# Conditioning rows loaded on GpSimd's queue into a buffer of their own, and reduced across four stages of a mixer block

## The chip, the cores and the metric

One core of one Trainium2 chip. The metric is the device time of one execution in microseconds (us), taken as the median of several runs. Engines: PE (TensorE), DVE (VectorE), ACT (ScalarE), POOL (GpSimd), SP (SyncE, which here only issues DMAs). Each engine runs its instructions in the order in which they stand in its own queue.

## The reference

One layer of a diffusion backbone. Input: 512 latent tokens of width 1024, 256 context tokens, and a conditioning vector c. What matters here:

```
mod = split(silu(c) @ w_ada + b_ada, 6)          # six vectors of 1024
h   = rms_norm(x) * (1 + mod[1]) + mod[0]         # the same for the context tokens
z, xbc, dt, cv, pool, gates = split(h @ w_in)
xbc = silu(conv5(xbc) + bias)                     # 1536 channels, 5 taps
y   = ssd_scan(xbc, dt) from the context's final states, both directions
y   = rms_norm(y * silu(z)) @ ssd_w_out
merged = sum over 3 branches of sigmoid(gates[b]) * branch[b]
x   = x + mod[2] * (merged @ w_out)
h   = rms_norm(x) * (1 + mod[4]) + mod[3]
x   = x + mod[5] * swiglu(h)
out = rms_norm(x)
```

Of the context tokens only xbc's first ten channel tiles and dt are needed, for the states from which the latent scan starts.

## The kernel before, in words

**Products.** Channels lie on the 128 partitions, tokens along the free axis. A unit of weights is a tile of 128 x 1024 fp32 (512 KB), eight blocks of 128 columns, and gives one output tile of 128 channels x 512 tokens. Every operand is kept as a pair hi, lo whose sum is the fp32 value, and `mm3` (L132 to L137) makes a product of three matmuls per block: hi by hi (L135), hi by lo (L136), lo by hi (L137). `load_unit` (L116 to L127) issues the DMA of a unit into one of three buffers `wr` (L113, on SP's queue), casts it to `whi` on ACT (L121) and takes the difference `wlo` on DVE (L123).

**Order.** A tile framework schedules the instructions by dependence and by a running priority. Code under `later(n)` gets a later priority, so that work of one stage can stand as filler in another; buffers of a pool (the last argument of `pt`) bound how far an instruction moves up.

**Stages.** Start, GLU and pool branch (to about 165 us); twelve xBC units; the SSD scan, with z and gate units as filler for PE; gates, layer norm of the convolution branch and its output units `wcv` (to 517.6 us); the units `wso` with the merge of the three branches; the units `wout` with the residual; the FFN from 605 us and its down projection.

**xBC unit** (loop at L721). 24 matmuls of 512 tokens for the latent tokens; in the first ten units 24 more of 256 for the context tokens, against `hc`, the context's pairs hi, lo of 128 x 256. ACT copies both results into a padded tile `pad` (slots C5, four of them), whose edges POOL clears (L727, L728, L734). `conv5` makes four taps on DVE (L669), ACT applies Silu, and the tail (`xbc_tail`, a generator) transposes the result on PE (L699, L703), scales a part on DVE (L706) and multiplies it on PE (L715). The tail of one unit stands inside the next but one. `conv_steps` adds taps of the 31 tap convolution (L403) as filler for DVE.

**Conditioning.** Chunks 2, 4 and 3 of mod are not needed until `wout` and later. `ada()` (L854 to L863) makes 128 values of them: it loads a tile of 512 KB of `wada` with `load_raw`, so into a shared buffer `wr` on SP's queue, and one DVE instruction (L861) multiplies it by silu(c) and sums along the free axis into a column of `mod_l`. 24 such calls stand in the gate units (4), the `wcv` units (4), the `wso` units (8) and the `wout` units (8). Eight more, of chunk 5, stand in the down projection.

**Merge.** In each `wso` unit m SP loads gate tile m (`ga`, L933) and the two spilled branch results (`mo`, L934) from DRAM, 512 KB each; DVE combines them with the product (L936 to L939) and splits the result for `wout`.

Of the kernel before, what the change touches and what calls it, by code (L numbers as in the profile page):

```python
# [8 lines left out]
F32 = mybir.dt.float32  # L9
F32R = mybir.dt.float32r  # L10
AF = mybir.ActivationFunctionType
ALU = mybir.AluOpType
P = 128
# [39 lines left out]
def hybrid_block(ctx, tc, x, cx, cck, cc, wad, wada, vec, prm, cst, inv, win, wdt, wcv, wpl, wso, wout, wgu, wdn, out):  # L53
# [78 lines left out]
    def mm3(o, w, col, rhs, first, last):  # L132
        hi, lo = w
        rh, rl = rhs
        PE.matmul(o, hi[:, col : col + P], rh, start=first, stop=False)  # L135
        PE.matmul(o, hi[:, col : col + P], rl, start=False, stop=False)  # L136
        PE.matmul(o, lo[:, col : col + P], rh, start=False, stop=last)  # L137
# [272 lines left out]
    def conv_steps(n, ins=None):  # L410
        with ExitStack() as st:
            st.enter_context(later(100000))
            if ins is not None:
                st.enter_context(tc.issue_after(ins.ins))
            while n and convs:
                if next(convs[0], 0) == 0:
                    convs.popleft()
                else:
                    n -= 1
# [87 lines left out]
    def ctx_norm():  # L507
        x3 = xc[:, 0:2, :].rearrange("p a (t n) -> p (a t) n", n=TC)
        nc.sync.dma_start(x3, cx)
        xs_c = [x3[:, t, :] for t in range(KT)]  # L510
        r = norm_sum(xs_c, TC)
        hq = [slot_h([P, 4, 2, TC], F32R) for _ in range(2)]
        for t in range(KT):
            h = hq[t // 4][:, t % 4]
            make_h(xs_c[t], r, m1_c[:, t : t + 1], mod_c[:, t : t + 1], h[:, 0, :], h[:, 1, :])
            hc.append((h[:, 0, :], h[:, 1, :]))

    def pool_all():
        plp, waiting = [], []
# [155 lines left out]
    def xbc_tail(i, pad):  # L675
# [17 lines left out]
        else:  # L693
# [23 lines left out]
                    )  # L717
            S.copy(pinit[:, :, i * P : (i + 1) * P], st[:, :TC].rearrange("p (d n) -> p d n", n=P))

    tails = []  # L720
    for q, i in enumerate((8, 9, 10, 11, 0, 1, 2, 3, 4, 5, 6, 7)):  # L721
        w = load_unit(win[I_XBC + q])
        o = mmp()
        for k in range(KT):
            mm3(o, w, k * P, hh[k], k == 0, k == KT - 1)
        pad = slot_c()
        nc.gpsimd.memset(pad[:, 0:2], 0.0)  # L727
        nc.gpsimd.memset(pad[:, 514:518], 0.0)  # L728
        S.copy(pad[:, 2:514], o)
        if i < 10:  # L730
            oc = mmp()
            for k in range(KT):
                mm3(oc[:, :TC], w, k * P, hc[k], k == 0, k == KT - 1)
            nc.gpsimd.memset(pad[:, 774:776], 0.0)  # L734
            S.copy(pad[:, 518:774], oc[:, :TC])
        conv_steps(CONV_STEPS_XBC[q], mark[-1])
        while len(tails) > TAILS_KEPT_XBC[q]:
            drain(tails.pop(0))
        tails.append(xbc_tail(i, pad))
        next(tails[-1], None)  # L740
# [99 lines left out]
            nc.sync.dma_start(yd[:, 4 * g : 4 * g + 4, zs], zc)  # L840
            yield

    silb = [None]

    def load_sil(t):
        nc.sync.dma_start(t, cc[0:1, :].to_broadcast([P, 1024]))
        tc.keep_in_program_order(S.activation(t, t, AF.Silu))
        silb[0] = t

    adas = deque()  # L850
    for i in range(24):
        adas.append(((2, 4, 3)[i // 8], i % 8))

    def ada(n=1):  # L854
        for _ in range(n):
            if not adas:
                return
            chunk, t = adas.popleft()
            raw = load_raw(wada[(chunk - 2) * 8 + t], 1024)
            i = chunk * 8 + t  # L860
            V.tensor_tensor_reduce(  # L861
                raw, raw, silb[0], 1.0, vc("b_ada", i), ALU.mult, ALU.add, mod_l[:, i : i + 1]
            )  # L863

    load_sil(f1.tile([P, 1024], F32, tag="sil1", name="sil1"))
    gens = [ssd_gen(0), ssd_gen(1)]
    for g in gens:
        next(g)
# [58 lines left out]
    for m in range(8):  # L927
        w = load_unit(wso[m])
        o = mmp()
        for k in range(KT):  # L930
            mm3(o, w, k * P, y_hl[k], k == 0, k == KT - 1)
        ga, mo = slot_a(), slot_c().rearrange("p (a b) -> p a b", b=T)
        nc.sync.dma_start(ga, gat[:, m])  # L933
        nc.sync.dma_start(mo, mrg[:, m])  # L934
        S.activation(ga, ga, AF.Sigmoid)
        V.tensor_tensor(mo[:, 1, :], mo[:, 1, :], ga[:, 1, :], ALU.mult)  # L936
        V.tensor_tensor(mo[:, 0, :], mo[:, 0, :], mo[:, 1, :], ALU.add)
        V.tensor_tensor(ga[:, 0, :], o, ga[:, 0, :], ALU.mult)
        V.tensor_tensor(mo[:, 0, :], mo[:, 0, :], ga[:, 0, :], ALU.add)  # L939
        mr = mo[:, 0, :]  # L940
        split(mg[m][0], mg[m][1], mr)
        ada(1)

    x1 = slot_x([P, KT, T])
    acc = pt(per, [P, T], "sum", 1)
# [51 lines left out]
    for m in range(nh):  # L997
        if m < 2:
            o = pair[m][1]
        else:  # L1000
            w, o = wout_tile(m)
            project(o, [(w, KT)], mg, whole[0])
        residual(m, o, mod_l[:, 16 + m : 17 + m], xp[m // 2][:, m % 2, :], whole[0], slot_m())
        prescale(m, whole[0])
        ada(2 - m // 3)
    last = [wout_tile(m) for m in range(nh, 8)]
    h2 = [(pt(per, [P, T], "hh", 8, F32R), pt(per, [P, T], "hl", 8, F32R)) for _ in range(KT)]

# [190 lines left out]
    hid = hs  # L1199

    acc = pt(per, [P, T], "sum", 1)
    for m in range(8):
        ada(1)
        o = mmp()
# [129 lines left out]
```

## Time and profile before

| | |
|---|---|
| median of 3 runs | 979.4 us (977.9 to 980.53) |
| the profiled execution | 976.52 us |
| span in its trace | 974.7 us |
| mean granted clock of PE in the span | 0.996 |
| PE busy | 948.8 us (97%) |
| DVE busy | 764.9 us (78%) |
| ACT busy | 492.2 us (50%) |
| POOL busy | 15.9 us (2%) |
| moved by DMA | 151.67 MB, 156 GB/s over the span |

The span is that of the instructions; the execution's own time is 1.8 us more. The median of the runs is 2.9 us above the profiled execution. A matmul's busy time in a row is its latency; matmuls overlap, so the step from one start to the next tells their rate. The granted clock is written as a share: 1.00 is 2.4 GHz and 0.50 is 1.2 GHz.

### The profile page before, as it was taken

The numbers are of one execution on the slowest core, as the hardware profiler recorded it, in microseconds if no ns is written. First come the engines' busy times: TensorE is split into PE (matmuls) and PEld (weight loads), VectorE is DVE, ScalarE is ACT, GpSimd is POOL, SyncE is SP. The second block draws the span as 40 slices with busy tenths as digits, with TensorE's granted clock in tenths as the row PEclk, the third lists the DMA queues.
The fourth block names the chain that finished last, engine by engine and source line by source line (L and its number), as shares of the span: only waits on it lengthen the run. The fifth ranks groups of instructions, "written<-read, shape, count | busy, mean of one in ns | idle before, by whom it ended". The sixth has DMA issues, their size and how long they took to land.

```text
span 974.7 us, 14173 instructions
## 1 busy us (share of the span) xinstructions
PE 948.8 (97%) x5420; PEld 803.6 (82%) x5420; DVE 764.9 (78%) x1165; ACT 492.2 (50%) x815; POOL 15.9 (2%) x58
## 2 busy tenths in 40 slices
PE   6999999999999999999999989999999999999996
PEld 4678888888887776777888769989999999888885
DVE  5589999967889999987876976999889888643333
ACT  5683597335445254644844434745555556432331
POOL 0000000000000000000000000000000000000000
PEclk9999999999999999999999999999999999999998
DMA  9753455321112346665578984223232323343422
GB/s 364 282 187 110 164 179 173 109 87 65 67 65 76 108 162 195 216 205 196 176 259 318 363 278 170 91 104 131 101 117 87 119 99 122 127 141 109 136 79 87
DMA packets 55492, 151.67 MB, mean 156 GB/s; under 512 B 5760, under 2 KB 16512, under 8 KB 54272
## 3 DMA queue, kind: packets, MB, share of 16 engines
q1 hardware_dynamic: 55424, 150.77, 44.6%
q8 instruction: 42, 0.69, 0.3%
q14 instruction: 26, 0.21, 0.1%
HBM read 134.43 MB, written 16.32 MB: 155 GB/s over the span
## 4 chain that ended last, share of the span: by engine, by line
PE 86%; DVE 7%; DMA 4%; ACT 2%; issue 1%; SPq 0%; DVEq 0%; ACTq 0%
PE mm L137 19%; PE mm L135 19%; PE mm L136 19%; PE mm L1122 10%; PE ps L1122 8%; PE mm L62 1%; DMA C<-mrg 1%; DVE wlo L123 1%; DVE A L403 1%; PE ps L1039 1%; PE ps L763 1%; PE y L825 1%; PE ps L62 1%; PE ps L715 1%; DMA wr<-in_wso_dram 1%
## 5 line engine op out<-in xcount | busy, mean ns | idle before, releaser
L135 PE MATMUL mm<-hh,whi 128*128 128x512 f32 (+1 forms) x612 | 242.4, 396 | 0.0
L137 PE MATMUL mm<-hh,wlo 128*128 128x512 f32 (+1 forms) x612 | 241.2, 394 | 0.5 <-DVE wlo L123 0.5
L136 PE MATMUL mm<-hl,whi 128*128 128x512 f32 x576 | 228.9, 397 | 0.0
L121 ACT CAST whi<-wr 128x1024 fp32r<-128x1024 f32 (+1 forms) x115 | 116.9, 1019 | 212.1 <-PE mm L136 167.4
L123 DVE TENSOR_TENSOR wlo<-wr,whi 128x1024 fp32r<-128x1024 f32 (+1 forms) x112 | 132.2, 1183 | 63.1 <-ACT whi L121 62.0
L137 PEld LDWEIGHTS mm<-hh,wlo 128*128 128x128 f32 x612 | 115.0, 188 | 28.3 <-issue 2.8
L135 PEld LDWEIGHTS mm<-hh,whi 128*128 128x128 f32 x612 | 115.1, 188 | 26.0 <-issue 1.7
L136 PEld LDWEIGHTS mm<-hl,whi 128*128 128x128 f32 x576 | 108.3, 188 | 25.0 <-issue 2.7
L403 DVE SCALAR_TENSOR_TENSOR A<-U,vec_t,A 128x504 f32<-128x504 f32 (+14 forms) x180 | 115.4, 684 | 0.1
L129 ACT CAST shi<-S 128x1024 fp32r<-128x1024 f32 x36 | 37.9, 1052 | 32.1 <-DVE S L1110 26.3
L1122 PE MATMUL mm<-T,shi 128*128 128x256 f32 x288 | 53.5, 283 | 0.0
L669 DVE SCALAR_TENSOR_TENSOR C<-C,vec_t,C 128x772 f32<-128x772 f32 (+1 forms) x48 | 46.9, 977 | 4.9 <-ACT C L667 2.4
L130 DVE TENSOR_TENSOR slo<-S,shi 128x1024 fp32r<-128x1024 f32 x36 | 44.1, 1225 | 5.8 <-ACT shi L129 5.7
L818 ACT ACTIVATE E<-E,sbias 128x128 f32<-128x128 f32 x128 | 40.0, 392 | 10.6 <-DMA E<-cumd 10.5
L1122 PEld LDWEIGHTS mm<-T,shi 128*128 128x128 f32 x288 | 44.8, 191 | 0.0
L129 ACT CAST whi<-wr 128x1024 fp32r<-128x1024 f32 (+1 forms) x36 | 30.0, 835 | 26.0 <-PE ps L1122 21.4
L861 DVE CUSTOM_DVE_ANT_0 wr<-wr,sil,vec_t 128x1024 f32<-128x1024 f32 x24 | 30.8, 1282 | 13.4 <-DMA wr<-in_wada_dram 13.4
L137 PE MATMUL mm<-H,wlo 128*128 128x256 f32 (+1 forms) x124 | 38.0, 307 | 2.9 <-DVE wlo L123 2.8
L1122 PE MATMUL mm<-T,slo 128*128 128x256 f32 x144 | 40.8, 284 | 0.0
L130 DVE TENSOR_TENSOR wlo<-wr,whi 128x1024 fp32r<-128x1024 f32 (+1 forms) x36 | 34.5, 958 | 7.6 <-ACT whi L129 6.0
L135 PE MATMUL mm<-H,whi 128*128 128x256 f32 (+1 forms) x124 | 37.8, 305 | 0.0
L136 PE MATMUL mm<-H,whi 128*128 128x256 f32 (+1 forms) x124 | 37.7, 304 | 0.0
(383 smaller groups left out, 2039.4 us busy)
## 6 DMA issues: line engine op xcount, KB each, us to landing
wr<-in_win_dram SPq DMA_DIRECT2D x62, 512.0 KB, 3.7
wr<-in_wgu_dram SPq DMA_DIRECT2D x44, 512.0 KB, 3.4
wr<-in_wada_dram SPq DMA_DIRECT2D x32, 512.0 KB, 4.0
E<-cumd SPq DMA_DIRECT2D x16, 512.0 KB, 5.3
wr<-in_wdn_dram SPq DMA_DIRECT2D x16, 512.0 KB, 3.9
X<-in_wad_dram SPq DMA_DIRECT2D x4, 1024.0 KB, 10.6
H<-in_wad_dram SPq DMA_DIRECT2D x4, 1024.0 KB, 11.2
mrg<-tmp SPq DMA_DIRECT2D x16, 256.0 KB, 4.0
```

Source lines behind the costliest of these rows:

```text
L121: S.copy(hi[:, :n], raw[:, :n])
L123: V.tensor_tensor(lo[:, :n], raw[:, :n], hi[:, :n], ALU.subtract)
L129: S.copy(dst_hi, src)
L130: V.tensor_tensor(dst_lo, src, dst_hi, ALU.subtract)
L135: PE.matmul(o, hi[:, col : col + P], rh, start=first, stop=False)
L136: PE.matmul(o, hi[:, col : col + P], rl, start=False, stop=False)
L137: PE.matmul(o, lo[:, col : col + P], rh, start=False, stop=last)
L403: V.scalar_tensor_tensor(accs[e][:, :, o], ins[e][:, :, q], vc("dw_w", (2 * j + e) * 31 + 15 + d), accs[e][:, :, o], ALU.mult, ALU.add)
L669: tap = V.scalar_tensor_tensor(a[:, 0:n], pad[:, k : n + k], vc("conv_w", i * 5 + k), a[:, 0:n], ALU.mult, ALU.add)
L818: S.activation(dec[d][:, j, :], dec[d][:, j, :], AF.Identity, bias=sbias[:, z, c : c + 1])
L861: V.tensor_tensor_reduce(raw, raw, silb[0], 1.0, vc("b_ada", i), ALU.mult, ALU.add, mod_l[:, i : i + 1])
L1122: PE.matmul(o[:, left], x[:, cs], rhs[k][y], start=first and k + n == 0, stop=k == 3 and n == 2, skip_group_check=True,)
```

## The change

1. `hc` now holds, for each block of the context, hi (128 x 256) and the whole pair hi, lo side by side (128 x 512). The context product of an xBC unit is then two matmuls per block: whi by the pair (512 columns, L761) and wlo by hi (256 columns, L762). The two halves of the result are added on DVE (L765) as the second goes into `pad`.
2. `ada()` moves ahead of the xBC units. It loads into a buffer `ar` of its own, of which there is one, on GpSimd's DMA queue (L743), and the reduce (L735) of one call is issued by the next call, before its load. Its 24 calls stand in nine xBC units, the gate units (4), the `wcv` units (4) and seven `wso` units. The eight calls of chunk 5 use the same buffer and queue.
3. In the `wso` units `ga` and `mo` are loaded on GpSimd's queue (L941, L942).

```diff
-            hc.append((h[:, 0, :], h[:, 1, :]))
+            hc.append((h[:, 0, :], h.rearrange("p a n -> p (a n)")))
...
+    loaded = []
+
+    def ada_rest():
+        while loaded:
+            i, raw = loaded.pop()
+            V.tensor_tensor_reduce(raw, raw, silb[0], 1.0, vc("b_ada", i), ALU.mult, ALU.add, mod_l[:, i : i + 1])
+
+    def ada(n=1):
+        for _ in range(n):
+            ada_rest()
+            if adas:
+                chunk, t = adas.popleft()
+                raw = pt(per, [P, 1024], "ar", 1)
+                nc.gpsimd.dma_start(raw, wada[(chunk - 2) * 8 + t])
+                loaded.append((chunk * 8 + t, raw))
...
             oc = mmp()
             for k in range(KT):
-                mm3(oc[:, :TC], w, k * P, hc[k], k == 0, k == KT - 1)
+                ks = slice(k * P, k * P + P)
+                PE.matmul(oc, w[0][:, ks], hc[k][1], start=k == 0, stop=False, skip_group_check=True)
+                PE.matmul(oc[:, :TC], w[1][:, ks], hc[k][0], start=False, stop=k == KT - 1, skip_group_check=True)
             nc.gpsimd.memset(pad[:, 774:776], 0.0)
             S.copy(pad[:, 518:774], oc[:, :TC])
+            V.tensor_tensor(pad[:, 518:774], oc[:, TC:], pad[:, 518:774], ALU.add)
         conv_steps(CONV_STEPS_XBC[q], mark[-1])
+        ada(q > 2)
...
-    def ada(n=1):
-        for _ in range(n):
-            if not adas:
-                return
-            chunk, t = adas.popleft()
-            raw = load_raw(wada[(chunk - 2) * 8 + t], 1024)
-            i = chunk * 8 + t
-            V.tensor_tensor_reduce(
-                raw, raw, silb[0], 1.0, vc("b_ada", i), ALU.mult, ALU.add, mod_l[:, i : i + 1]
-            )
...
-        nc.sync.dma_start(ga, gat[:, m])
-        nc.sync.dma_start(mo, mrg[:, m])
+        nc.gpsimd.dma_start(ga, gat[:, m])
+        nc.gpsimd.dma_start(mo, mrg[:, m])
...
-        ada(1)
+        ada(m < 7)
+        if m == 7:
+            ada_rest()
...
-        ada(2 - m // 3)
...
+    ada(1)
     for m in range(8):
         ada(1)
```

The scheduler does not leave the calls where the code has them. Three places show it.

DVE in one xBC unit, before. C is the padded tile or the taps' sum, W the scaled part of the tail, A and U the 31 tap convolution:

```order
L706 TENSOR_TENSOR W_2070<-ps_2067,wdec 128x256
L123 TENSOR_TENSOR wlo_2271<-wr_2268,whi_2270 128x1024
L706 TENSOR_TENSOR W_2070<-ps_2067,wdec 128x256
L669 SCALAR_TENSOR_TENSOR C_315_2079<-C_309_2028,vec_t,C_315_2079 128x772 x4
L403 SCALAR_TENSOR_TENSOR A_457<-U_782,vec_t,A_457 128x8x53
L403 SCALAR_TENSOR_TENSOR A_457<-U_785,vec_t,A_457 128x8x53
L403 SCALAR_TENSOR_TENSOR A_457<-U_782,vec_t,A_457 128x8x52
L403 SCALAR_TENSOR_TENSOR A_457<-U_785,vec_t,A_457 128x8x52
L706 TENSOR_TENSOR W_2161<-ps_2158,wdec 128x256
```

The same place after the change; the reduces are the ISA rows with `ar`, and the ISA row behind each hands on its sum:

```order
L123 TENSOR_TENSOR wlo_2246<-wr_2243,whi_2245 128x1024
L765 TENSOR_TENSOR C_311_2015<-mm_2019,C_311_2015 128x256
L706 TENSOR_TENSOR W_2053<-ps_2050,wdec 128x256 x2
L735 ISA ar_3063,mod_l<-ar_3063,sil_1680,vec_t 128x1024
L735 ISA mod_l 128x1
L669 SCALAR_TENSOR_TENSOR C_318_2062<-C_311_2015,vec_t,C_318_2062 128x772 x4
L735 ISA ar_3202,mod_l<-ar_3202,sil_1680,vec_t 128x1024
L735 ISA mod_l 128x1
L403 SCALAR_TENSOR_TENSOR A_457<-U_782,vec_t,A_457 128x8x53
L403 SCALAR_TENSOR_TENSOR A_457<-U_785,vec_t,A_457 128x8x53
L123 TENSOR_TENSOR wlo_2333<-wr_2330,whi_2332 128x1024
```

Two reduces now stand in the unit, one between the tail (L706) and the taps (L669) of its convolution. In DVE's whole order 21 of the 24 reduces stand between the last rows of the pool branch and the end of the xBC tails, and the other three among the first rows of the SSD scan; none is left in the gate, `wcv`, `wso` or `wout` units.

PE at the border of two xBC units, before, with the tail's transposes (L699, L703):

```order
L136 MATMUL mm_2032<-H_617,whi_1999 128x256
L137 MATMUL mm_2032<-H_617,wlo_2000 128x256
L699 MATMUL ps_2061<-ident,C_304_1990 128x128 x4
L703 MATMUL ps_2067<-ident,C_304_1990 128x128 x2
L135 MATMUL mm_2092<-hh_81,whi_2088 128x512
L136 MATMUL mm_2092<-hl_82,whi_2088 128x512
L137 MATMUL mm_2092<-hh_81,wlo_2089 128x512
L715 MATMUL ps_2073<-W_2070,W_1676 128x128 x2
```

The same place after the change:

```order
L761 MATMUL mm_2104<-H_617,whi_2071 128x512
L762 MATMUL mm_2104<-H_617,wlo_2072 128x256
L135 MATMUL mm_2162<-hh_81,whi_2158 128x512
L136 MATMUL mm_2162<-hl_82,whi_2158 128x512
L137 MATMUL mm_2162<-hh_81,wlo_2159 128x512
L135 MATMUL mm_2162<-hh_83,whi_2158 128x512
L699 MATMUL ps_2131<-ident,C_318_2062 128x128 x4
L703 MATMUL ps_2137<-ident,C_318_2062 128x128 x2
L136 MATMUL mm_2162<-hl_84,whi_2158 128x512
```

The transposes stand four matmuls into the next unit here; in the units that follow, 8 to 12.

POOL in the xBC units after the change, where before it had only the clearings of the pads:

```order
L743 DMA ar_2390<-in_wada_dram 128x1024
L754 MEMSET C_303_1948 128x2
L755 MEMSET C_303_1948 128x4
L763 MEMSET C_303_1948 128x2
L743 DMA ar_2483<-in_wada_dram 128x1024
L754 MEMSET C_311_2015 128x2
L755 MEMSET C_311_2015 128x4
L763 MEMSET C_311_2015 128x2
L743 DMA ar_2570<-in_wada_dram 128x1024
L743 DMA ar_3063<-in_wada_dram 128x1024
```

The single buffer lets each DMA start only after the reduce of the tile before. The clearings of a unit's pad stand behind such DMAs. The first DMA, of `ar_1898`, stands at the head of POOL's queue, before the first clearings of the pool branch, and waits for nothing.

## Rows read from the trace of the kernel before

**Rows 1.** The page's first part: busy time, share, instructions of each engine.

```profile
PE 948.8 (97%) x5420; PEld 803.6 (82%) x5420; DVE 764.9 (78%) x1165; ACT 492.2 (50%) x815; POOL 15.9 (2%) x58
```

**Rows 2.** Windows: stretch, its us, busy of PE, PEld, DVE, ACT, POOL, clock, DMA share, GB/s.

```profile
165.00:320.00 155.00, 155.00 (x843) 131.32 (x842) 130.32 (x178) 66.86 (x101) 2.31 (x35) 1.00 0.23 79
320.00:460.00 140.00, 137.56 (x665) 101.56 (x665) 126.48 (x204) 71.06 (x148) 10.18 (x8) 1.00 0.55 182
...
517.60:565.00 47.40, 45.29 (x195) 35.89 (x193) 40.21 (x61) 22.41 (x26) 0.00 (x0) 1.00 0.94 347
565.00:605.00 40.00, 38.63 (x194) 32.51 (x195) 26.87 (x39) 16.36 (x23) 0.00 (x0) 0.96 0.71 245
```

**Rows 3.** Waits of PE: line, awaited, us in total, times, longest.

```profile
PE mm L137 <- DVE wlo L123: 3.3, 3, 2.0
PE ps L763 <- DVE W L761: 1.6, 1, 1.6
```

**Rows 4.** Timeline of PE around 563 us: start, us, instruction, idle before.

```profile
561.88 0.39 PE L135 MATMUL mm<-hh,whi 128*128 128x512 f32 x1
562.11 0.39 PE L136 MATMUL mm<-hl,whi 128*128 128x512 f32 x1
...
563.03 0.39 PE L136 MATMUL mm<-H,whi 128*128 128x512 f32 x1
565.38 0.50 PE L137 MATMUL mm<-H,wlo 128*128 128x512 f32 x1 [1.96 <-DVE wlo L123]
```

**Rows 5.** Windows, as rows 2: the stretch after that stall.

```profile
566.50:569.80 3.30, 3.30 (x10) 2.58 (x9) 2.72 (x4) 0.80 (x1) 0.00 (x0) 0.52 0.78 284
```

**Rows 6.** DMA issues of 505 to 610: issue, count, KB each, median us to landing.

```profile
wr<-in_wada_dram SPq DMA_DIRECT2D x16, 512.0 KB, 4.6
...
C<-mrg SPq DMA_DIRECT2D x7, 512.0 KB, 6.8
```

**Rows 7.** Chain that ended last, 505 to 612: start, length, what.

```profile
519.51 6.09 DMA C<-mrg
...
543.71 5.76 DMA wr<-in_wso_dram
...
578.96 3.48 DMA wr<-in_wout_dram
```

**Rows 8.** DVE by line and form, 500 to 610: count, busy us, mean ns, idle before.

```profile
L861 DVE CUSTOM_DVE_ANT_0 wr<-wr,sil,vec_t 128x1024 f32<-128x1024 f32 x17 | 21.8, 1282 | 10.8 <-DMA wr<-in_wada_dram 10.8
```

**Rows 9.** Timeline of DVE through one xBC unit: start, us, instruction, idle before.

```profile
282.66 0.42 DVE L706 TENSOR_TENSOR W<-ps,wdec 128x256 f32<-128x256 f32 x1 [1.60 <-PE ps L703]
283.00 1.22 DVE L123 TENSOR_TENSOR wlo<-wr,whi 128x1024 fp32r<-128x1024 f32 x1
284.13 0.42 DVE L706 TENSOR_TENSOR W<-ps,wdec 128x256 f32<-128x256 f32 x1
284.65 4.27 DVE L669 SCALAR_TENSOR_TENSOR C<-C,vec_t,C 128x772 f32<-128x772 f32 x4
288.83 1.16 DVE L403 SCALAR_TENSOR_TENSOR A<-U,vec_t,A 128x392 f32<-128x392 f32 x2
...
292.69 0.42 DVE L706 TENSOR_TENSOR W<-ps,wdec 128x256 f32<-128x256 f32 x1 [1.37 <-PE ps L703]
```

**Rows 10.** DMA issues of 195 to 320, as rows 6.

```profile
wr<-in_win_dram SPq DMA_DIRECT2D x14, 512.0 KB, 3.5
```

**Rows 11.** Timeline of PE, end of a context product.

```profile
251.46 0.28 PE L136 MATMUL mm<-H,whi 128*128 128x256 f32 x1
251.58 0.28 PE L137 MATMUL mm<-H,wlo 128*128 128x256 f32 x1
```

**Rows 12.** Chain that ended last, 0 to 30, as rows 7.

```profile
1.65 5.33 DMA X<-in_wad_dram
```

**Rows 13.** DMA view, 0 to 26 us: GB/s in 40 slices.

```profile
GB/s 0 0 30 131 323 93 403 365 429 321 391 375 394 410 410 407 407 463 432 466 397 384 416 479 403 429 429 429 466 403 397 391 473 416 429 416 416 454 403 435
```

**Rows 14.** POOL by line and form, whole run, as rows 8.

```profile
L795 POOL TENSOR_TENSOR W<-X,cbd 128x512 f32<-128x512 f32 x8 | 10.2, 1272 | 146.5 <-DVE cbd L791 105.3 <-issue 29.7 <-DMA yd<-W 11.5
```

More of the change, by code (lines that the diff above doesn't have):

```diff
@@ L718, in xbc_tail, with load_sil @@
             S.copy(pinit[:, :, i * P : (i + 1) * P], st[:, :TC].rearrange("p (d n) -> p d n", n=P))
+    silb = [None]
+    def load_sil(t):
+        nc.sync.dma_start(t, cc[0:1, :].to_broadcast([P, 1024]))
+        tc.keep_in_program_order(S.activation(t, t, AF.Silu))
+        silb[0] = t
+    adas = deque()
+    for i in range(24):
+        adas.append(((2, 4, 3)[i // 8], i % 8))
+    loaded = []
[11 more added lines that the diff above has]
+                loaded.append((chunk * 8 + t, raw))
+    load_sil(f1.tile([P, 1024], F32, tag="sil1", name="sil1"))
     tails = []
@@ L841, in ssd_gen @@
             yield
[L843 to L852, printed above, removed]
-    def ada(n=1):
-        for _ in range(n):
-            if not adas:
-                return
-            chunk, t = adas.popleft()
-            raw = load_raw(wada[(chunk - 2) * 8 + t], 1024)
-            i = chunk * 8 + t
-            V.tensor_tensor_reduce(
-                raw, raw, silb[0], 1.0, vc("b_ada", i), ALU.mult, ALU.add, mod_l[:, i : i + 1]
-            )
-    load_sil(f1.tile([P, 1024], F32, tag="sil1", name="sil1"))
     gens = [ssd_gen(0), ssd_gen(1)]
```

## The prediction

> **What bounds the kernel now.** I read the page's busy shares first: PE works 948.8 us, 97% of the span [rows 1], so it is the bound, and the change can win only where PE waits, where its clock falls, or where it does less. The waits of PE come next. Apart from the wait for the first weights at the start, only two releasers in the part that the change touches cost more than 1.2 us: the difference `wlo` of a weight unit, 3.3 us in three waits, and a tile W in the SSD scan, 1.6 us [rows 3]. The windows by stage then show who is nearly full behind PE [rows 2]. In the xBC stage (165 to 320) DVE works 130.3 of 155 us and the DMA engines are 23% busy; in the SSD scan DVE works 126.5 of 140 us; in the `wso` stage it is the DMA engines that are full, 94% at 347 GB/s, and in the `wout` stage they are still at 71%.
>
> The three waits for `wlo` all lie in those last two stages. The timeline shows the longest: a matmul at 563.03 us, the next at 565.38, where the step is 0.23 us otherwise [rows 4]. In the stretch behind it the granted clock is 0.52 for 3.3 us, the lower level, and is back before 570 us [rows 5]. The chain through these stages runs over transfers: a branch result `C<-mrg` of 6.1 us, a weight unit of `wso` of 5.8 us, one of `wout` of 3.5 us [rows 7]. Between 505 and 610 us, 16 loads of `wada` (4.6 us each) stand beside the merge's loads (6.8 us) on the same engines [rows 6], and on DVE their reduces stand in the order ahead of `wlo`.
>
> **The change, part by part.** The sum starts from the profiled execution, 976.52 us. That run is 2.9 us below the median of the runs (979.4), so I carry the difference over to the median at the end.
>
> *The start.* The first load of a conditioning row is now at the head of POOL's queue and waits for nothing. The transfers of the start already run at some 410 GB/s [rows 13] and the end's chain begins with one of them [rows 12]. Another 512 KB at that rate is 0.52 MB / 410 GB/s = 1.3 us. It costs nothing if it lands in a gap and 1.3 us if PE's first weights wait for all of it. Most of the start's chain hangs on transfers, so I take **+1.2** (0 to 1.3).
>
> *The context product.* A block had three matmuls of 256 columns with 0.12 us from start to start [rows 11]; it now has one of 512 (0.23, rows 4 give the step) and one of 256 (0.12). That saves 3 x 0.12 - 0.35 = 0.01 us per block; with 8 blocks in 10 units, **-0.9**. Ends: 0 and -1.
>
> *DVE in the xBC stage.* In are 21 reduces of 1.28 us [rows 8], 26.9 us, and ten additions at the 0.42 us of a DVE instruction of that size [rows 9], 4.2 us. Out are nine taps of the 31 tap convolution that the new order leaves to the SSD scan, at 0.58 us [rows 9], 5.2 us. So 130.3 + 26.9 + 4.2 - 5.2 = 156.2 us of work must go through a stage in which PE would need 155 - 0.9 = 154.1: **DVE is over by 2.1 us**. Before, DVE also waited 1.4 to 1.6 us per unit for the transposes [rows 9]. These now stand 4 to 12 matmuls into the next unit, 0.9 to 2.8 us later, but with a reduce and the addition ahead of the tail, so I expect nearly all of that wait to be covered. It is a loop, though: taps, Silu, transposes, tail, next taps. Whatever DVE loses comes back to PE as a wait at the transposes. I take **+2.5**. The ends: 0, if the lead that `wlo` has over PE soaks it up, and 2.1 + 6 x 1.5 = +11, if the old waits remain.
>
> *The single buffer.* A load can start only when the reduce before it is done, and the next reduce waits for it on DVE, in order, with the taps of the same unit behind it. Between two reduces DVE has the four taps, 4.18 us from 284.65 to 288.83 [rows 9], or the other items of a unit. Its work without the reduces is 1.13 + 2 x 0.34 + 4.18 + 2 x 0.58 + 0.42 = 7.6 us, so with two reduces in a unit the gaps are 3.8 us each, and about ten gaps are of 3.8 to 5.0 us. How long the round trip takes from the end of a reduce over POOL's issue to the landing is in no row, since before no data moves on POOL's queue. The nearest is SP's load of the same size in the same stretch, 3.5 us [rows 10]; far up lie the 4.6 and 6.8 us of the full stage [rows 6]. The stretch is nearly empty of other transfers, so I take it near the lower row, a little over 4 us with POOL's part, which the gaps just cover: **0**. At 5.5 us it is ten times 1.1, +11.
>
> *POOL's queue.* Behind those loads stand the clearings of the next pad. A late clearing would hold the first step of a unit's convolution, which waits for the context product anyway. It costs 0 as long as the round trip fits; otherwise it is part of the price above.
>
> *The SSD scan.* Three reduces leave and three others come; nine taps come, 5.2 us: 126.5 + 5.2 = 131.7 of 140 us. There is room on the whole, but DVE is dense where PE already waited 1.6 us for it [rows 3]. I take **+1** (-1.6 to +4).
>
> *Gates and `wcv`.* Five reduces leave; PE waits for nothing there: 0.
>
> *`wso` and `wout`.* All 16 reduces (20 us of DVE) and 8 MB of transfers leave, and SP's queue holds little but weights, which then come as early as three buffers allow. That takes the three waits (3.3 us), about 0.15 us of restart behind each (2.35 - 0.23 - 1.96 at the longest, rows 4), and the lower clock, 3.3 x (1 - 0.52) = 1.6 us [rows 5]: **-5.4**. The merge's loads stay on the same 16 engines, so a remainder can survive: -2 at the small end, -6 at the large.
>
> *FFN.* The eight late reduces sit where PE waits for no DVE work of theirs: 0.
>
> Sum: 1.2 - 0.9 + 2.5 + 0 + 1 - 5.4 = **-1.6**, so 974.9 us against the profiled execution and 979.4 - 1.6 = **977.8** against the median.
>
> **The rivals.**
>
> *The xBC stage absorbs it all (chance 0.26).* `wlo` is made well ahead of its matmul, and PE waits nowhere in 165 to 320 before. If DVE's reserve covers 2 us, and the denser SSD scan loses nothing, the sum is 1.2 - 0.9 - 5.4 = -5.1: 974.3 us. Against it: DVE's work alone is over PE's, and the loop closes every unit.
>
> *The round trip is longer than the gaps (0.25), slower.* Place: the reduce between L706 and the taps. Each gap shorter than the round trip stops DVE, then the taps, the Silu and PE's transposes. It decides from about 4.8 us: ten gaps of 4.4 us on average then cost 4 us and the sum passes +2.4. At 5.5 us the sum is -1.6 + 11 = +9.4, 988.8 us; at 4.9 us it is some 983. For it: five units in a row have two reduces, and POOL must see the reduce's end, issue, and let 16 engines fetch. Against it: the 3.5 us of SP's loads.
>
> *The queue moves nothing (0.09).* The merge's loads are still late, since two queues feed the same engines, and a wait for `wlo` or the merge remains with its clock drop: the gain shrinks to 2, the sum is +1.8, 981.2 us, within the noise. Against it: a third of the stage's bytes are gone. The Trainium skill (DMA: Bandwidth & Descriptors, "Issuing engines are not separate DMA queues") says that transfers begun by different engines run on the same 16 DMA engines, and only the issuing time is saved; no run shows it here yet.
>
> *DVE keeps GpSimd from starting loads (0.02).* If a load could not start while DVE works, DVE would have to go idle at each reduce, and 21 round trips of 3.5 us would be open, +73 us. Against it: POOL's own multiplications take 1.27 us on average [rows 14] in a stage where DVE is 90% busy. The Trainium skill (SBUF — State Buffer, the box on DVE blocking DMA under "SBUF: two separate sides") has this rule, for loads of GpSimd's queue under DVE's two-port modes; most of DVE's work here reads two tensors at about one element per ns, so I give it little.
>
> **How the numbers follow.** A measurement here tells 0.3%, 2.9 us, from no change: faster is below 976.5, slower above 982.3. My forecast (0.38) has its own range of 975 to 981 and lies below 976.5 in a third of it. Faster: 0.26 and 0.12, 0.38. Slower: the long round trip with 0.24, the trap with 0.02 and 0.02 of the rest, 0.28. The same: 0.34. For 8 in 10 the range starts at 972.5 (full gain, -1.6 from the SSD scan) and reaches to 987, which takes in round trips to 5.3 us.
>
> **What would show it.** Right: no wait of PE for `wlo` L123 between 517 and 605 us and a clock of 1.00 there; about 8 MB fewer in these stages; DVE over 97% busy in the xBC stage with waits of PE at L699 that sum to 2 to 3 us; waits of DVE for the `ar` loads of under 2 us in all. The forecast is wrong if DVE waits for `ar` by several us per unit (then the round trip was longer than 4.8 us), if PE's first matmul is not later, or if the `wso` stage still waits.

## The result and the profile after

The changed kernel takes 984.88 us (median of 4 runs, 984.2 to 987.04) against 979.29 for the kernel before on the same chip (4 runs): a ratio of 1.0068, with a 95% interval of 1.0052 to 1.0084. It is slower by 0.7%, where the likeliest forecast was 977.8. The profiled execution is the 987.04 one; its span is 985.3 us, 10.6 more than before, where the medians differ by 5.6, so some 5 us of the gap between the two traces is the luck of the two executions, and only the large parts of it are read below.

One gain that was worked out is in the trace, and larger than forecast. The stages `wso` and `wout` run without a wait of PE: the last two windows of the changed kernel, read as rows 2, show PE busy for all of them at the full clock, where before it lost 2.1 and 1.4 us in two windows, the second at a clock of 0.96 [rows 2].

```profile
165.00:320.00 155.00, 148.50 (x722) 122.07 (x721) 138.59 (x203) 64.99 (x97) 13.13 (x56) 0.98 0.42 137
320.00:460.00 140.00, 135.81 (x631) 100.11 (x631) 133.85 (x213) 66.93 (x140) 11.84 (x11) 0.99 0.56 177
520.00:570.00 50.00, 50.00 (x220) 41.13 (x219) 26.82 (x36) 22.11 (x27) 7.68 (x15) 1.00 0.75 260
570.00:610.00 40.00, 40.00 (x201) 34.05 (x200) 25.21 (x34) 19.00 (x27) 0.26 (x1) 1.00 0.55 184
```

The loss is in the first two rows: PE is idle for 6.5 of 155 us in the xBC stage, with a clock of 0.98, and for 4.2 of 140 in the scan, and DVE is busy for only 138.6 us of a stage that was forecast as overfull. DVE's waits from 195 to 330 us (us in total, times, longest) point to the reason:

```profile
DVE ar L735 <- DMA ar<-in_wada_dram: 11.1, 10, 4.3
```

The first two units hold the largest of them. DVE's timeline of the changed kernel there (start, us, instruction, idle before):

```profile
202.38 0.08 DVE L735 DVE_READ_ACCUMULATOR2_ANT mod_l<- 128x1 f32 x1
202.38 1.26 DVE L403 SCALAR_TENSOR_TENSOR A<-U,vec_t,A 128x440 f32<-128x440 f32 x2
207.91 1.28 DVE L735 CUSTOM_DVE_ANT_0 ar<-ar,sil,vec_t 128x1024 f32<-128x1024 f32 x1 [4.28 <-DMA ar<-in_wada_dram]
209.13 0.08 DVE L735 DVE_READ_ACCUMULATOR2_ANT mod_l<- 128x1 f32 x1
209.13 1.22 DVE L123 TENSOR_TENSOR wlo<-wr,whi 128x1024 fp32r<-128x1024 f32 x1
210.26 0.42 DVE L765 TENSOR_TENSOR C<-mm,C 128x256 f32<-128x256 f32 x1
213.42 1.28 DVE L735 CUSTOM_DVE_ANT_0 ar<-ar,sil,vec_t 128x1024 f32<-128x1024 f32 x1 [2.74 <-DMA ar<-in_wada_dram]
214.63 0.08 DVE L735 DVE_READ_ACCUMULATOR2_ANT mod_l<- 128x1 f32 x1
214.63 4.26 DVE L669 SCALAR_TENSOR_TENSOR C<-C,vec_t,C 128x772 f32<-128x772 f32 x4
```

And POOL's, which issues the loads:

```profile
202.76 0.53 POOL L743 DMA_DIRECT2D ar<-in_wada_dram  x1 [33.93 <-DVE mod_l L735]
209.50 0.53 POOL L743 DMA_DIRECT2D ar<-in_wada_dram  x1 [6.21 <-DVE mod_l L735]
```

A reduce hands on its sum at 202.46; POOL starts the next load at 202.76, is busy with it for 0.53 us, and the reduce that needs it starts at 207.91: a round trip of 5.45 us. The next one, from 209.21 to 213.42, is 4.2. Between the two reduces DVE has 1.26 us of work, then 1.6. The first taps of the whole stage (L669) stand behind the third reduce and start at 214.63, 14.8 us after the start of the pool branch's last instructions on DVE; in the trace before it was 9.7. In the next unit the reduces stand among the taps, and the delay reaches PE at the first transposes:

```profile
226.42 0.40 PE L137 MATMUL mm<-hh,wlo 128*128 128x512 f32 x1
230.87 1.11 PE L687 MATMUL ps<-ident,bt 128*128 128x128 f32 x4 [4.05 <-ACT bt L682]
```

```profile
229.80:236.40 6.60, 5.53 (x16) 4.64 (x17) 6.60 (x11) 4.46 (x8) 0.83 (x6) 0.50 0.57 173
390.20:393.40 3.20, 3.20 (x22) 2.51 (x21) 2.11 (x3) 0.00 (x0) 0.00 (x0) 0.50 0.79 270
```

PE stands still for 4.05 us and then works for 5.5 us at a granted clock of 0.50, the lower of its two levels, which costs another 2.8 us (an estimate: half of that busy time). All of PE's waits from 195 to 470 us:

```profile
PE ps L794 <- DVE W L792: 4.2, 2, 2.5
PE ps L687 <- ACT bt L682: 4.1, 1, 4.1
PE ps L699 <- ACT C L695: 1.9, 3, 0.8
PE ps L715 <- DVE W L706: 0.5, 1, 0.5
```

Four stops at the tails (L699, L715) add 2.4 us. The largest line is in the scan: two waits for a tile W, 4.2 us against 1.6 before [rows 3], with the lower clock again behind the longer one (390.2 to 393.4). Ahead of that late W stand, among other work, six taps of the 31 tap convolution on DVE, work of the kind that the new order leaves to the scan:

```profile
381.74 3.69 DVE L403 SCALAR_TENSOR_TENSOR A<-U,vec_t,A 128x456 f32<-128x456 f32 x6
...
388.29 0.68 DVE L792 TENSOR_TENSOR W<-X,wdec 128x512 f32<-128x512 f32 x1
```

So the loss has two places: the xBC units, the second of them above all, and the scan, which takes about a third (2.6 us more of waiting and some 1.6 of low clock). That the taps cause the second is argued from the order; no run moves them alone.

To place the whole difference, I cut each trace at four marks, the starts of the last DVE instructions of the pool branch, of ACT's last copy of a `wcv` result, of DVE's last residual of `wout`, and of PE's last sum for the final norm; the 8.3 to 9.0 us behind that are left out. The lengths are read from the timelines; in brackets, the difference to before. Runs e1 to e16 are told below.

| us | to the pool's end | xBC, scan, gates, wcv | wso, wout | FFN, down |
|---|---|---|---|---|
| before | 196.9 | 321.7 | 96.3 | 351.2 |
| after | 199.9 (+3.0) | 333.8 (+12.1) | 89.7 (-6.6) | 353.4 (+2.2) |
| e1 no loads | 199.9 (+3.0) | 317.9 (-3.8) | 89.8 (-6.6) | 353.0 (+1.9) |
| e2 conditioning only | 200.3 (+3.4) | 330.8 (+9.1) | 89.7 (-6.7) | 353.0 (+1.9) |
| e3 context only | 198.1 (+1.2) | 319.5 (-2.2) | 98.5 (+2.2) | 351.2 (0.0) |
| e4 merge only | 198.4 (+1.5) | 321.3 (-0.4) | 102.5 (+6.2) | 351.6 (+0.4) |
| e5 held to unit 3 | 198.1 (+1.2) | 342.4 (+20.8) | 89.7 (-6.7) | 353.6 (+2.5) |
| e6 one per unit | 197.5 (+0.6) | 320.9 (-0.8) | 95.6 (-0.7) | 353.1 (+2.0) |
| e7 clean start | 197.0 (+0.1) | 330.2 (+8.5) | 90.5 (-5.8) | 354.6 (+3.4) |
| e8 as e5, merge on SP | 198.4 (+1.6) | 341.4 (+19.7) | 89.7 (-6.6) | 354.6 (+3.5) |
| e9 spread | 198.1 (+1.3) | 321.2 (-0.5) | 95.7 (-0.6) | 353.1 (+1.9) |
| e10 as e9, merge on SP | 198.7 (+1.8) | 320.7 (-0.9) | 96.3 (0.0) | 351.2 (+0.1) |
| e11 loads on SP | 198.7 (+1.8) | 327.2 (+5.6) | 89.7 (-6.7) | 354.5 (+3.4) |
| e12 reduces late | 197.6 (+0.7) | 342.4 (+20.8) | 89.7 (-6.6) | 353.1 (+1.9) |
| e13 the same on SP | 198.3 (+1.4) | 332.1 (+10.5) | 90.6 (-5.7) | 353.2 (+2.1) |
| e14 as e13, merge on SP | 196.7 (-0.2) | 331.3 (+9.7) | 89.7 (-6.7) | 353.0 (+1.8) |
| e15 xBC and gates, SP | 198.5 (+1.6) | 319.3 (-2.4) | 89.7 (-6.7) | 351.2 (0.0) |
| e16 the same, POOL | 197.5 (+0.6) | 324.9 (+3.2) | 89.7 (-6.7) | 351.2 (0.0) |

Small differences are not to be leaned on: kernels that leave the start untouched (e3, e4) also stand 1.2 to 1.5 us above the trace before at the pool's end, and the cause of the 2 us in the FFN, which come and go with the order of the late part, was not looked for.

### The profile page after: what moved, and what is told of

Read it like the earlier page. It is cut to its first block, busy times and chain, and to the rows that moved or that the text cites. A ratio compares the mean times of both kernels' runs of the same rounds, so it can differ in the third digit from the quotient of the medians.

```text
span 985.3 us, 14045 instructions
## 1 busy us (share of the span) xinstructions
PE 952.6 (97%) x5340; PEld 803.0 (81%) x5340; DVE 763.0 (77%) x1175; ACT 491.5 (50%) x815; POOL 42.2 (4%) x106
## 4 chain that ended last, share of the span: by engine, by line
PE 75%; DVE 9%; issue 9%; DMA 4%; ACT 1%; POOL 0%; SPq 0%; DVEq 0%; POOLq 0%; ACTq 0%
PE mm L135 17%; PE mm L137 16%; PE mm L136 16%; PE mm L1131 8%; PE ps L1131 6%; DMA ar<-in_wada_dram 2%; PE mm L62 1%; DVE C L669 1%; DVE A L403 1%; PE ps L1048 1%; PE ps L62 1%; PE y L856 1%; DMA wr<-in_wgu_dram 1%; DVE wlo L123 1%; DMA X<-in_wad_dram 1%
## 5 line engine op out<-in xcount | busy, mean ns | idle before, releaser
L403 DVE SCALAR_TENSOR_TENSOR A<-U,vec_t,A 128x504 f32<-128x504 f32 (+14 forms) x180 | 118.1, 692 | 0.1
L669 DVE SCALAR_TENSOR_TENSOR C<-C,vec_t,C 128x772 f32<-128x772 f32 (+1 forms) x48 | 46.4, 974 | 1.7 <-ACT C L667 1.2
L129 ACT CAST whi<-wr 128x1024 fp32r<-128x1024 f32 (+1 forms) x36 | 30.1, 835 | 24.8 <-PE ps L1131 19.9
L735 DVE CUSTOM_DVE_ANT_0 ar<-ar,sil,vec_t 128x1024 f32<-128x1024 f32 x24 | 30.7, 1281 | 11.4 <-DMA ar<-in_wada_dram 11.4
L743 POOL DMA_DIRECT2D ar<-in_wada_dram x32 | 17.2, 536 | 295.9 <-DVE mod_l L735 268.8
L761 PE MATMUL mm<-H,whi 128*128 128x512 f32 x80 | 28.5, 396 | 0.0
L1131 PE MATMUL ps<-T,shi 128*128 128x256 f32 x144 | 27.2, 285 | 0.7 <-ACT shi L129 0.4
```

The lines of the kernel that those rows point to most:

```text
L129: S.copy(dst_hi, src)
L403: V.scalar_tensor_tensor(accs[e][:, :, o], ins[e][:, :, q], vc("dw_w", (2 * j + e) * 31 + 15 + d), accs[e][:, :, o], ALU.mult, ALU.add)
L669: tap = V.scalar_tensor_tensor(a[:, 0:n], pad[:, k : n + k], vc("conv_w", i * 5 + k), a[:, 0:n], ALU.mult, ALU.add)
L735: V.tensor_tensor_reduce(raw, raw, silb[0], 1.0, vc("b_ada", i), ALU.mult, ALU.add, mod_l[:, i : i + 1])
L1131: PE.matmul(o[:, left], x[:, cs], rhs[k][y], start=first and k + n == 0, stop=k == 3 and n == 2, skip_group_check=True,)
```

## The experiments

Theory A: DVE waits, in order, for loads into one buffer, and what that costs lies in the units where little work stands between two reduces. Theory B: DVE simply has more work than PE. Ratios are to the kernel before on the same chip, with their 95% intervals.

**One part at a time.** e2 is the kernel before with the `ada` edits only, e3 with the context product only, e4 with this only:

```diff
-        nc.sync.dma_start(ga, gat[:, m])
-        nc.sync.dma_start(mo, mrg[:, m])
+        nc.gpsimd.dma_start(ga, gat[:, m])
+        nc.gpsimd.dma_start(mo, mrg[:, m])
```

> The kernel before with only the move of the conditioning rows (own single buffer, GpSimd's queue, reduces deferred); context product and the merge's loads as before. Theory A: the whole loss is here, start +2.6, xBC some +10, less the wso gain of 5 to 6: 984 to 987 us. Theory B: without the ten additions and with the old loop DVE is 4 us lighter, 979 to 982.

> The kernel before with only the context product of two matmuls per block and its addition on DVE. Theory A: PE saves 0.9 us, DVE's 0.4 us per unit lies in its idle 1.5: 978 to 979.5 us. Theory B: the addition lengthens the loop taps, Silu, transposes, tail: 981 to 984.

> The kernel before with only the merge's loads (gates and spilled results) on GpSimd's queue. If the stall in wso and wout came from the order of SP's queue, this alone gives most of the gain there: 974 to 976 us. If it came from the conditioning loads and their reduces ahead of wlo on DVE, nearly nothing: 978 to 980.

Measured: e2 982.6 us, 1.0045 (1.0033 to 1.0057), between its two expectations; e3 976.72 us, 0.9982 (0.997 to 0.9994), better than both of its own; e4 984.47 us, 1.0067 (1.0056 to 1.0079). The conditioning part carries most of the loss in the second column, 9.1 of 12.1 us, and already has the whole gain in `wso` and `wout`. The context product alone gains 1.8 us by its ratio (0.6 to 3), which agrees with the 0.9 forecast. The parts do not simply add up: with product and merge on top of e2, the change is 2.3 us slower than e2 by the ratios. The merge's move alone costs 6 us in its stage, which neither of its two expectations had. In e4 SP's queue, freed of the merge's loads, keeps to its old pairs of a weight unit and a conditioning row, and DVE stands before conditioning rows with `wlo` and the merge behind them, for 19.9 us in all between 500 and 610 us against 10.8 before [rows 8]. PE later stops for a merged tile (timelines of e4):

```profile
525.10 1.29 DVE L861 CUSTOM_DVE_ANT_0 wr<-wr,sil,vec_t 128x1024 f32<-128x1024 f32 x1 [5.76 <-DMA wr<-in_wada_dram]
...
526.31 1.22 DVE L123 TENSOR_TENSOR wlo<-wr,whi 128x1024 fp32r<-128x1024 f32 x1
532.71 1.29 DVE L861 CUSTOM_DVE_ANT_0 wr<-wr,sil,vec_t 128x1024 f32<-128x1024 f32 x1 [5.17 <-DMA wr<-in_wada_dram]
```

```profile
571.64 0.40 PE L137 MATMUL mm<-W,wlo 128*128 128x512 f32 x1
575.54 0.50 PE L135 MATMUL mm<-W,whi 128*128 128x512 f32 x1 [3.50 <-ACT W L129]
```

So e4 shows the same in-order wait for a conditioning row in another stage. That the waits around 530 us make the tile late that PE stops for at 575 us is argued, not shown. Once the rows are out of the stage, the queue is worth little: e8 against e5 and e14 against e13, below.

**The waits without the loads.** e1 keeps 24 reduces at places near those of the change, each anchored behind an instruction on DVE (one instead of three ahead of the first taps), and gives them something to read that needs no load. It leaves out the conditioning values of these chunks, so it measures time only:

```diff
+            with tc.high_priority(), tc.issue_after(ins.ins):
+                V.tensor_tensor_reduce(
+                    held[0], silb[0], silb[0], 1.0, vc("b_ada", i), ALU.mult, ALU.add, mod_l[:, i : i + 1]
+                )
```

> The changed kernel with the 24 reduces of chunks 2, 4 and 3 at nearly the same places in DVE's order (each anchored behind the tap, addition or wlo it follows there), but reading silu(c) instead of a loaded row; the 24 loads are left out except one at the start, so the conditioning values of these chunks are not computed. DVE's work stays, its waits for ar go. Theory A (the waits for the single buffer's round trip in the first two xBC units, and the lower clock behind PE's stop there, are the loss): the stop of 4 us before L687 and the 3.5 us at the lower clock go, 976 to 979 us. Theory B (DVE simply has more work than PE in the xBC stage): no better than 983.

Measured: 971.25 us, 0.9938 (0.9924 to 0.9952), 13 us below the change and better than theory A asked. DVE is even busier in the xBC stage, 147.8 of 155 us, and PE is idle there for 0.06 (windows of e1); from 195 to 460 us PE waits for 1.3 us in all:

```profile
165.00:320.00 155.00, 154.94 (x776) 129.44 (x775) 147.75 (x218) 69.18 (x103) 2.54 (x36) 1.00 0.25 81
```

```profile
PE ps L813 <- DVE W L811: 0.8, 1, 0.8
PE ps L813 <- ACT tmp L385: 0.5, 1, 0.5
```

Theory B falls for the xBC stage: 23 reduces up to its last tail cost PE nothing when nothing is waited for. e1 is no clean removal of the waits alone: it also takes 12 MB out of the DMA engines and has two of the first three reduces behind the first taps, which start 9.8 us after the pool branch as before. The next runs keep the loads.

**The start.** e7 holds only the first load behind the clearing of unit 0's pad (`tc.issue_after` around the call); DVE's order stays.

> The changed kernel with only the first conditioning load held behind the first pad's clearing of unit 0, so that the start is free of it; the order on DVE is that of the changed kernel. Theory A: the start gets its 1.5 to 2.5 us back and the stop in the first units stays: 982 to 983.5 us. If the start's delay is not that load's: 984.5 to 985.5.

Measured: 981.61 us, 1.0041 (1.0025 to 1.0057). By the ratios that is 2.6 us better than the change, but the two intervals leave 0.4 to 4.9. PE's first product tells more exactly what the load at the head of POOL's queue costs (timelines of the kernel before, of the change, of e7):

```profile
7.12 1.93 PE L62 MATMUL ps<-X,cct 128*32 128x256 f32 x16 [7.12 <-DMA X<-in_wad_dram]
```

```profile
8.64 1.46 PE L62 MATMUL ps<-X,cct 128*32 128x256 f32 x9 [8.64 <-DMA X<-in_wad_dram]
```

```profile
7.38 1.93 PE L62 MATMUL ps<-X,cct 128*32 128x256 f32 x16 [7.38 <-DMA X<-in_wad_dram]
```

It starts at 8.3 to 8.6 us in the three kernels with that load (the change, e1, e2) and at 7.05 to 7.54 us in all the others: about 1.5 us. The stop before L687 stays, at 2.6 us in e7's trace.

**The queue.** e11 issues the same loads with `nc.sync.dma_start`; DVE's first reduces stand as in the change.

> The changed kernel with the conditioning loads issued on SP's queue, still into the single buffer. If the queue of GpSimd makes the round trip long: the wait per load falls by about 1 us and the stop in the first units with it, 979 to 982 us. If a single buffer is the cause whatever the queue, and SP's weights now stand behind loads that wait for a reduce: no better than 983.

Measured: 976.61 us, 0.9982 (0.9968 to 0.9996), 8 us below the change by the ratios, more than either expectation. Some 1.3 us of that are the start, since no load is at the head of POOL's queue (PE's first product at 7.33 us). Its profiled execution, at 980.84 us, is the slowest of its runs. The timeline of DVE in e11 at the place shown above:

```profile
201.18 0.08 DVE L735 DVE_READ_ACCUMULATOR2_ANT mod_l<- 128x1 f32 x1
...
206.06 1.28 DVE L735 CUSTOM_DVE_ANT_0 ar<-ar,sil,vec_t 128x1024 f32<-128x1024 f32 x1 [3.62 <-DMA ar<-in_wada_dram]
207.27 0.08 DVE L735 DVE_READ_ACCUMULATOR2_ANT mod_l<- 128x1 f32 x1
...
210.99 1.28 DVE L735 CUSTOM_DVE_ANT_0 ar<-ar,sil,vec_t 128x1024 f32<-128x1024 f32 x1 [2.17 <-DMA ar<-in_wada_dram]
```

The two round trips are 4.8 us (201.26 to 206.06) and 3.65 (207.35 to 210.99), each 0.6 shorter than on GpSimd's queue: SP issues 0.03 us after the sum, not 0.3, and the landing takes a median of 3.5 us instead of 3.8 (the tile `ar` from 190 to 330 us in the two traces, 3.3 to 4.6 against 3.6 to 5.0). All of DVE's waits for `ar` together are 7.0 us in 4 instead of 11.4 in 11. PE still stops before L687 for 3.1 us, but the clock is at its lower level behind it for about half as long as in the change, and the later stops at L699 are one instead of three:

```profile
228.40:231.60 3.20, 3.20 (x11) 2.81 (x12) 3.20 (x5) 3.10 (x6) 0.00 (x0) 0.50 0.31 104
231.80:240.00 8.20, 8.20 (x41) 6.86 (x40) 7.70 (x13) 2.80 (x4) 0.34 (x6) 1.00 0.45 146
```

**Moving the reduces later.** e5 holds each unit's load behind that unit's pad (first load in unit 3), e8 is e5 with the merge on SP; e12 holds every reduce behind unit 1's last tap and the first load behind unit 0's pad, e13 holds the reduces in the same way with the loads on SP's queue, e14 also has the merge on SP.

```diff
+            with tc.issue_after(mark[8].ins):
+                V.tensor_tensor_reduce(raw, raw, silb[0], 1.0, vc("b_ada", i), ALU.mult, ALU.add, mod_l[:, i : i + 1])
```

> The changed kernel with each xBC unit's conditioning load held behind the clearing of that unit's pad on POOL: the first load leaves in unit 3 instead of at the start, one reduce per xBC unit, the other 16 reduces in the SSD scan and the gates. Theory A (loss = waits in the first two units, and about 2 us from the load at the start): both go, 970 to 975 us, unless the 16 reduces crowd DVE in the SSD scan, then up to 978. Theory B (DVE's work, wherever it lies in xBC and scan): still 981 or more.

> As e5_held_unit3, with the merge's loads back on SP's queue. If GpSimd's queue for them is worth nothing once the conditioning loads are out of the stage: within 1 us of e5_held_unit3. If it costs as in the run of it alone: 2 us or more below e5; if it is what made the stage run without waits: 2 us or more above.

> The changed kernel (GpSimd's queue, single buffer) with the first load held behind unit 0's first pad clearing and every reduce held behind unit 1's taps: 16 reduces in the xBC units from unit 2, 8 in the scan. The first two units' taps then wait for no load. Theory A (the stop before the first transposes and the low clock behind it are 7 us, the start 3): 973 to 977 us. If instead the longer round trip of GpSimd's queue in all later units is the larger part: 978 to 982.

> As e12_late_pool with the conditioning loads on SP's queue. If only the first two units mattered: the same as e12 within 1.5 us. If GpSimd's round trip costs in every unit: 2 us or more faster than e12, 970 to 974.

> As e13_late_sp with the merge's loads on SP's queue too, so that nothing is on GpSimd's. If the merge's queue is worth nothing once the conditioning loads are out of its stage: the same as e13 within 1.5 us.

Measured: e5 993.72 us, 1.0163 (1.0142 to 1.0185); e8 994.96, 1.017 (1.0146 to 1.0195); e12 992.88, 1.0151 (1.0138 to 1.0165); e13 983.47, 1.0054 (1.004 to 1.0067); e14 981.84, 1.0043 (1.003 to 1.0056). All three times that were expected (e5, e12, e13) are missed, on the slow side. What was expected of pairs held: e8 is within 1 us of e5 and e14 within 1.5 of e13 by the ratios, and e13 is 9 us faster than e12. The first taps are back in time (10 to 11 us after the pool branch in e5, e12 and e13) and PE no longer stops before L687, so the first units are mended; but the reduces that no longer fit into xBC go into the SSD scan: 13 of them up to its end in e5, 8 in e12, 7 in e13, where the change had 3. There the loss comes back. PE's two largest waits of e12 from 195 to 480 us, and its window of the scan:

```profile
PE ps L798 <- DVE W L796: 9.0, 4, 3.6
PE y L847 <- DVE W L840: 5.1, 1, 5.1
```

```profile
320.00:460.00 140.00, 128.00 (x578) 93.40 (x576) 125.76 (x200) 61.95 (x132) 12.96 (x14) 0.96 0.56 182
```

The scan's tiles W are late on DVE, PE loses 12 us in 140, and the granted clock is 0.96. This is not theory B as it stands: DVE is busy for 125.8 us there, no more than the 126.5 before [rows 2], and waits itself (7.2 us for ACT, 3.2 us for `ar`, between 310 and 480 us). The order ahead of W seems to count, and it was not taken apart. With loads on SP (e13) the second column loses half as much, and PE's waits for DVE there are 8.7 us. The merge's queue (e8 against e5, e14 against e13) is worth no more than the intervals show.

**One reduce per unit.** e6 holds each reduce behind the `wlo` of the unit in which its call stands (in the trace 8 in xBC, 9 in scan, gates and `wcv`, 7 in the `wso` stage); e9 moves the calls out of the `wso` stage, but two reduces still land behind the last `wcv` copy, and e10 is e9 with the merge on SP.

> As e5_held_unit3, and each reduce also held behind the wlo of the unit that its call stands in, so 8 reduces in xBC, 8 in gates and wcv, 8 in the wso stage. Theory A: no waits in xBC; in the wso stage eight loads and reduces come back, but not ahead of the weights on SP's queue: 970 to 976 us. If reduces beside the merge on DVE are what made the old stall, it returns: 975 to 979.

> The changed kernel with each load held behind the clearing of its xBC unit's pad and each reduce behind the wlo of its unit, and the calls moved: seven or eight in xBC from unit 4, one per gate pair (8), one per wcv unit (8), none in the wso stage; merge loads on GpSimd's queue. Theory A with what the other runs added (a reduce costs nothing where it does not wait and DVE has room: about one per xBC unit, few in the scan, many in gates and wcv): no stop in xBC, no stop in wso and wout, clean start: 970 to 973 us. If one more reduce per gate pair crowds the scan: 974 to 977.

> As e9_spread_pool with the merge's loads on SP's queue. If the queue of the merge's loads does not matter once the conditioning loads are gone from the stage: within 1 us of e9. If SP's order makes weights late behind them: 2 us or more above.

Measured: e6 976.34 us, 0.9987 (0.9973 to 1.0001); e9 977.93, 0.9996 (0.9984 to 1.0007); e10 974.92, 0.9965 (0.9948 to 0.9982). e6 is in the upper of its two ranges, e9 just above both of its own, and e10 is 3 us faster than e9 by the ratios, where its expectations were no difference or slower. All are better than the change, but eight calls in the `wcv` units, one per unit of 4.1 us, wait for the single buffer again: DVE's waits for `ar` from 460 to 570 us are 15.6 us in e9 and 20.4 in e10. With the two reduces that are left there, the gain in `wso` and `wout` is gone (-0.6 and 0.0 us). PE stops for 3.2 us in each: in e10 at 533 us, right behind a reduce that waited 6.9 us for its load; in e9 near 557 us for a weight tile that ACT casts late, because it stands before a gate tile of the merge, so that this stop hangs on a load of the merge, which is on GpSimd's queue in e9.

**Where there is room.** e15 combines what held: 16 reduces in xBC behind unit 1's taps, none in the scan, 4 in the last gate units and 4 in `wcv`, none in the `wso` stage, all loads on SP. e16 has the conditioning loads on GpSimd's queue, held out of the start.

```diff
+            with tc.issue_after(mark[8].ins if len(adas) > 7 else unit_mark[0].ins):
...
-        ada(q > 2)
+        ada(2 * (q > 3))
...
-            ada(m % 2)
+            ada(m > 3)
...
-        ada(m < 7)
-        if m == 7:
-            ada_rest()
+        ada_rest()
```

> Context product of the change; conditioning loads into the single buffer on SP's queue, merge's loads on SP's queue; 16 reduces in the xBC units, held behind unit 1's taps, none in the scan, 8 in late gate and wcv units, none in the wso stage. Theory A as it stands now (a reduce is free in xBC where its load is not awaited, dear in the scan, and the wso stage is clean without conditioning loads): xBC at most 1.5 us of waits, scan and gates as before or better, wso and wout 6.6 us less: 969 to 973 us. If reduces in late gates and wcv cost as in the scan: 975 to 979.

> As e15_xbc_and_gates_sp with the conditioning loads on GpSimd's queue, the first held behind unit 0's first pad clearing. If GpSimd's queue lengthens every round trip by some 0.6 us and that reaches PE: 2 to 5 us above e15. If the queue mattered only in the first two units and the scan: within 1.5 us of e15.

Measured: e15 968.74 us, 0.9893 (0.988 to 0.9907), just under its first range; e16 973.06 us, 0.9946 (0.993 to 0.9962), as its first expectation had it. **e15 is the fastest of all, 1.1% below the kernel before and 1.7% below the change by the ratios.** PE's waits from 195 to 610 us, of e15 and then of e16:

```profile
PE ps L701 <- ACT C L697: 1.0, 1, 1.0
PE ps L797 <- DVE W L795: 0.8, 2, 0.4
PE ps L797 <- ACT tmp L385: 0.6, 1, 0.6
```

```profile
PE ps L701 <- ACT C L697: 3.8, 4, 1.6
PE ps L800 <- DVE W L798: 1.1, 2, 0.6
PE ps L800 <- ACT E L855: 1.0, 1, 1.0
PE y L849 <- DVE W L842: 0.8, 2, 0.5
```

With nearly the same places, GpSimd's queue costs 5 us by the ratios: DVE waits for `ar` 8 times for 8.6 us instead of 3 times for 2.3, and four stops at the transposes (3.8 us) stand against one (1.0). That fits the loop that the prediction described, taps, Silu, transposes, closing on a late load. No run gave `ar` a second buffer, which would be the direct test of the single one.

## Why the prediction was wrong

- **The step that failed is the single buffer, priced at 0.** It set a round trip of a little over 4 us against gaps of 3.8 to 5.0 us, worked out for a late unit with a tail. The round trip is 4.2 to 5.5 us on GpSimd's queue, and the gaps of the first two units are 1.3 and 1.6: they have no tail, and the order puts three reduces ahead of the first taps. The order was known; the sum read it in a late unit only. DVE's waits for `ar` were forecast at under 2 us and are 11.4. PE's stop of 4.05 us before L687 and the 2.8 us of low clock behind it stand where the term had 0.
- **The slower rival had the mechanism and not the place.** It put the wait between tail and taps of the later units and asked for 4.8 us of round trip; the largest waits are in the first units, where the gap is 1.3 us and a trip of 4.2 us would do. With hindsight its chance of 0.25 was low. The measured time lies inside the range, but on the other side of no change.
- **DVE in the xBC stage, +2.5, was mis-sized.** e1 has DVE fuller still and PE waits nowhere: the two stages together are 3.8 us shorter there, where the terms for context product, xBC and scan summed to +2.6. PE's 2.4 us at the tails in the change have the size of this term, by luck: DVE is busy for 89% of the stage, not the 97% that the term rests on. DVE's sum of work was the wrong measure: a stage that it fills to 95% costs PE nothing as long as nothing that PE needs is late.
- **The scan, +1, was mis-sized too:** the waits for W rose by 2.6 us, and the lower clock behind the longer one adds some 1.6 (half of the 3.2 us at 0.50), together at the upper end of its range (-1.6 to +4).
- **The start, +1.2, was about right:** PE's first product is 1.5 us later, a little over the upper bound of 1.3; e7's ratio gives 2.6 (0.4 to 4.9).
- **`wso` and `wout`, -5.4, was right** in cause and a little small: -6.6 in the change and within 0.1 of that in nine of the eleven other runs that have no conditioning row in these stages (-5.8 and -5.7 in e7 and e13); with rows left there it is gone (e6, e9, e10). The merge on GpSimd's queue gains nothing (e8 against e5, e14 against e13), e10 without it is 3 us faster than e9, and alone it loses 6 us. The Trainium skill says that transfers begun by different engines run on the same 16 DMA engines, and that issuing from several saves only the issuing time (DMA: Bandwidth & Descriptors, "Issuing engines are not separate DMA queues"). These runs agree in that no gain came of the second queue; none shows which engines the transfers used.
- **The context product, -0.9**, gave 1.8 us by e3's ratio (0.6 to 3), which does not exclude 0.9.
- **That DVE keeps GpSimd from starting loads** did not happen: POOL issues 0.3 us after the sum with DVE at work, and `ar` lands in a median of 3.8 us. The Trainium skill's box on it (SBUF — State Buffer, under "SBUF: two separate sides") concerns DVE's two-port modes; no run here tests one against a load.
- Not settled: the 2 us in the FFN; what in the order makes W late in the scan, and with it why e12 loses twice as much in its second column as e13 with nearly the same places.

## What to carry to other kernels

A load into a single buffer whose consumer stands in order on a shared engine holds that engine for round trip minus gap at each place (here 5.45 - 1.26 and 4.2 - 1.6 us, for waits of 4.28 and 2.74), so list the work between every two consumers in the scheduled order, the first units above all, not the mean over a stage. Work moved out of a crowded stage should be pinned to stages that have room (here 16 in xBC, 8 in gates and `wcv`, none in the scan); a scheduler that pulls it all forward turns a gain of 6.6 us into a loss of 5.6. Judge such a move part by part: here one of the three parts gained nothing, and the queue chosen for another cost 5 us in e16 against e15.

## What was not expected of the hardware

- A stop of PE cost more than itself, and not in proportion: behind the 4.05 us before L687 the granted clock was 0.50 from 229.8 to 236.4 us; behind the 3.1 us at the same place in e11 it was 0.50 from 228.4 to 231.6, and behind the 2.6 us in e7 from 227.0 to 230.3.
- The round trip over GpSimd's queue was 0.6 us longer than over SP's, half of it from the issue (0.3 us after the release against 0.03) and half from the landing (3.8 against 3.5 us); 24 such trips in nearly the same places were worth 5 us of the kernel (e16 against e15, by the ratios).
- DVE at 147.8 of 155 us beside PE at 154.94 cost PE nothing (e1).
